# Four stored gates multiplied right after the conformer, and a fifth in its own projection

## The chip, the cores and the metric

The program runs on one core of one Trainium2 chip. The metric is the device time of one execution in microseconds, lower is better; it is given as the median of repeated runs. Matrix products run on TensorE (PE, its weight loads PEld), elementwise work on VectorE (DVE), ScalarE (ACT) and GpSimd (POOL), and nearly all transfers are issued by SyncE (SP), in one queue that is worked through in order. An engine executes its own instructions in order as well.

## What is computed

The reference is a trunk of two layers over 1024 latent tokens and 256 context tokens, 1024 channels wide. The change concerns the merge in layer 0, the even mixer:

```python
z, xbc, dt, glu, gate = split(h @ w_in, EVEN_SIZES)      # for the latents and for the context
ya = ssd_branch(z, xbc, dt, ...)                         # bidirectional Mamba-2
...
yb = conformer_conv(glu, cv_w, cv_b, cv_ln_g, cv_ln_b) * jax.nn.silu(gate)
return jnp.concatenate([ya, yb], axis=-1) @ w_out
```

`conformer_conv` is a gated depthwise convolution over time, a layer norm over the channels and a Silu. So `yb` is a product of two 1024-channel arrays over 1280 tokens: the conformer's result and the Silu of the gate's projection.

## The kernel before

All arrays of this stage stand channel-major: a tile of 128 channels by 1280 tokens (256 of the context, 1024 latents), eight tiles for 1024 channels. `SLICES` cuts the tokens into pieces of 512, 512 and 256. Matrix products are made in three passes of a high and a low part each (`zh`, `zl`, `hhi`, `hlo` and the like), so each weight is loaded raw, rounded on ACT into the high part (L158) and subtracted on DVE into the low part (L159).

`inproj0` does the in-projection of layer 0 and all that can be done beside it. A scheduler then sets the order of the instructions on each engine, and that order is fixed in the program. The parts that matter here, as the code has them:

- **The early gates.** The string `seq` interleaves the projections of the conformer's input (`glu`, whose convolutions run on POOL and DVE) with those of the SSD input and with five gates, channel tiles 4, 5, 6, 7 and 2 (`early`, L1270). Four stand in `seq`. `gate_early` (L1273 to L1280) projects a gate, takes its Silu on ACT (L1277) and stores it to DRAM, `gs_d` (L1278), because the conformer's result it belongs to does not exist yet.
- **The conformer** (L900 to L937) normalises the eight convolved tiles `cv` in place, slice after slice: mean, squares (POOL adds half of them, L922), the reciprocal root on POOL (`rstd_of`, L1544 and L1545), a product on DVE (L936) and the final Silu on ACT (L937). The eight tiles are done with the last of its slices. Its channel sum `csum` (L1321) lies in the one buffer of the pool `aq`, tag "accq", which the POOL convolutions used before.
- **The z blocks.** `zblocks((0, 1))` makes the first two column blocks of z beside the conformer; then comes the fifth early gate, `gate_early(2)`; then `ecf.close()` gives the memory of `aq` and of the conformer's pool back.
- **dt and the backward state.** `dt_prep` turns the dt columns into decays and stores two tables of rows, `rA_d` and `rB_d` (L1494). `ssd_back` walks ten chunks backwards: load the token-major chunk (`xtok`, 640 KB, L1508), weigh it on DVE (L1512), two matmuls (`bst`, L1532), the state `Hb` on POOL and DVE (L1528, L1536), and a store of each state (L1523).
- **The third z block**, `zblocks((2,))`: four weight quarters through two raw buffers (`wr`, L1150), split into a new pool `zp`, then ten token tiles of 24 matmuls (L171) each.
- **The last gates** (L1400). `gate(i)` runs for 3, 0, 1 and then for 4, 5, 6, 7, 2. The first three are projected: 72 matmuls, then per slice Silu (L1392), product (L1393), store to `yb_d` (L1394). For the five stored ones each slice is loaded from `gs_d` (L1385), multiplied on POOL (L1386) and stored to `yb_d` (L1387), through the four buffers of the tag "th". Between gates the raw weights `wb` of the out-projection are loaded (L1404).
- **The out-projection of layer 0.** It first reads the context's part of `yb_d` (`yl0`, L1407), splits eight weight tiles (`woh` on ACT, `wol` on DVE, `split_wo`), and multiplies (L1001) in step with the SSD chunks, whose row table `rB_d` is read into `rst` and copied on ACT (L1584).

The kernel's functions with the profile's line numbers:

Of the kernel before, what the change touches and what calls it, by code (L numbers as in the profile page):

```python
# [7 lines left out]
F32 = mybir.dt.float32  # L8
FR = mybir.dt.float32r
AF = mybir.ActivationFunctionType  # L10
ALU = mybir.AluOpType
# [3 lines left out]
P = 128  # L15
# [4 lines left out]
T = L + C  # L20
NT = T // P
SLICES = ((256, 768), (768, 1280), (0, 256))
# [88 lines left out]
class Kern:  # L111
# [1072 lines left out]
    def inproj0(self, hhi, hlo, cv, xbc_d, zs_d, gs_d, dtr, vwh, yb_d, xt_d, hb_d, s0, first):  # L1184
        tc, nc, A = self.tc, self.nc, self.A
        W = A["wch0"]
        e, wp, tq = self.e_in, self.wp, self.tq
        first, banks, emb = first
        ecf = ExitStack()
        aq = ecf.enter_context(self.pool(name="aq", bufs=1))  # L1190
# [19 lines left out]
        th = [[] for _ in range(8)]  # L1210
# [56 lines left out]

        order = [0, 1, 2, 3, 4, 5, 6, 7]
        seq = "gggggggxsxsxsxsxxxxxxxxg"
        early = (4, 5, 6, 7, 2)  # L1270
        g = x = ge = 0

        def gate_early(i):  # L1273

            def ev(ps, a, b):
                t = tq.tile([P, 512], F32, name="th", tag="th")
                nc.scalar.activation(t[:, :b - a], ps, AF.Silu)  # L1277
                nc.sync.dma_start(gs_d[i, :, a:b], t[:, :b - a])  # L1278

            self.proj_ch(wp, W[28 + i], hhi, hlo, ev)  # L1280
# [13 lines left out]
        em = ExitStack()  # L1294
# [29 lines left out]
            nc.gpsimd.tensor_tensor(csum[:, :T], csum[:, :T], cv[i][:, :T], op=ALU.add)  # L1324
        self.conformer(cv, csum, ecf)

        def token_major(xq, c, h):

            xc = xq.tile([P, 5, P], F32, name="xcT")
            nc.sync.dma_start(xc, xbc_d[5 * h:5 * h + 5, :, c * P:(c + 1) * P].rearrange("k p t -> p k t"))  # L1330
            xt = xq.tile([P, 5 * P], F32, name="xtok")
            for a, n in ((0, 3), (3, 2)):
                ps = self.bank("ms")
                for k in range(n):
                    nc.tensor.transpose(out=ps[:, k * P:(k + 1) * P], in_=xc[:, a + k], identity=self.ident)
                nc.scalar.copy(xt[:, a * P:(a + n) * P], ps[:, :n * P])
            nc.sync.dma_start(xt_d[c][:, 640 * h:640 * h + 640], xt)
# [31 lines left out]
                            nc.sync.dma_start(zs_d[t, :, 352 * j - 32:352 * j + 320], zs[:, :352])  # L1369
                assert not xq or not todo  # L1370

        zblocks((0, 1))
        gate_early(2)
        ecf.close()
        self.s0 = s0.__enter__()
        self.dt_prep(dtr)
        self.ssd_back(xt_d, hb_d)
        zblocks((2,))
        em.close()

        def gate(i):
            if i in early:
                for a, b in SLICES:
                    gt = tq.tile([P, 512], F32, name="gs", tag="th")
                    nc.sync.dma_start(gt[:, :b - a], gs_d[i, :, a:b])  # L1385
                    nc.gpsimd.tensor_tensor(gt[:, :b - a], cv[i][:, a:b], gt[:, :b - a], op=ALU.mult)  # L1386
                    nc.sync.dma_start(yb_d[a][i], gt[:, :b - a])  # L1387
                return

            def ev(ps, a, b):  # L1390
                gt = tq.tile([P, 512], F32, name="gs", tag="th")
                nc.scalar.activation(gt[:, :b - a], ps, AF.Silu)  # L1392
                nc.gpsimd.tensor_tensor(gt[:, :b - a], cv[i][:, a:b], gt[:, :b - a], op=ALU.mult)  # L1393
                nc.sync.dma_start(yb_d[a][i], gt[:, :b - a])  # L1394

            self.proj_ch(wp, W[28 + i], hhi, hlo, ev)

        ewl = self.ewl = ExitStack()
        wl = ewl.enter_context(self.pool(name="wl", bufs=1, side="right"))
        wb = [(k, wl.tile([P, D], F32, name=f"wb{k}", tag=f"wb{k}"), (wl, f"wb{k}")) for k in range(1, 8)]  # L1400
        for n, i in enumerate((3, 0, 1, 4, 5, 6, 7, 2)):
            gate(i)
            if n:
                nc.sync.dma_start(wb[n - 1][1], A["wout0"][8 + n])  # L1404
        we = ewl.enter_context(self.pool(name="we", bufs=1, side="right"))
        y = wl.tile([P, 8, P], F32, name="yl0", tag="wb0")
        nc.sync.dma_start(y, yb_d[256][:, :, :P].rearrange("k p t -> p k t"))  # L1407
# [271 lines left out]
```

## Time and profile before

| | us |
|---|---|
| three runs | 2196.39, 2198.22, 2204.89 |
| median | 2198.22 |
| the profiled execution | 2200.34 |
| its span | 2198.6 |
| PE busy | 2054.9 (93%) |
| PEld busy | 1630.2 (74%) |
| DVE busy | 1348.8 (61%) |
| ACT busy | 991.9 (45%) |
| POOL busy | 979.8 (45%) |

The profiled execution lies 2.1 us above the median of the runs, and 1.7 us of it lie outside its span. All times in the views count from the span's start. The shares are means over the whole span, in which stages with quite different limits follow each other; the stage around the change, from 540 to 1088 us, is read from the windows and timelines below. "Before <- X" in a row names what ended the engine's idle time ahead of the instruction.

### The profile page before, as it was taken

To read this page: it belongs to the slowest core of one execution; us is meant where nothing else is said; L and a number is where in the kernel's file an instruction comes from. 1 tells how busy PE (TensorE), PEld (TensorE's weight loads), DVE (VectorE), ACT (ScalarE), POOL (GpSimd) and SP (SyncE) were. 2 spreads that over 40 slices of the span, in tenths; PEclk is the share of its full clock that TensorE was granted. 3 is DMA by queue.
4 is the path that set the end of the run, shared out by engine and by line. 5 is a ranking of instruction groups with operands and counts; after the bars stand their busy time and mean duration, and the time that the engine had idled before them with its cause. 6 is when DMAs were issued, how large, how long until landed. Compare 5 with 4: busy or idle time off the path is not lost.

```text
span 2198.6 us, 28297 instructions
## 1 busy us (share of the span) xinstructions
PE 2054.9 (93%) x10636; PEld 1630.2 (74%) x10636; DVE 1348.8 (61%) x1889; ACT 991.9 (45%) x1549; POOL 979.8 (45%) x654
## 2 busy tenths in 40 slices
PE   7999999999979929999899999999999999899997
PEld 6888888889767716665488788888777676676675
DVE  6788896758445036667776321422566767676677
ACT  6455677533352122224234323233656767655510
POOL 0198999700112254546431113822445555434453
PEclk9999999999989969999899999999999999899998
DMA  8011122236637464464243422522311212534463
GB/s 306 30 39 39 51 79 85 96 129 213 218 106 250 169 221 149 146 214 157 98 159 125 134 70 82 179 99 80 99 49 51 59 52 57 159 92 126 122 182 130
DMA packets 158994, 269.33 MB, mean 123 GB/s; under 512 B 18901, under 2 KB 98385, under 8 KB 158601
## 3 DMA queue, kind: packets, MB, share of 16 engines
q1 hardware_dynamic: 157432, 264.01, 36.8%
q0 software_dynamic: 1280, 3.26, 0.5%
q8 instruction: 83, 1.36, 0.3%
q14 instruction: 55, 0.44, 0.1%
q10 hardware_dynamic: 144, 0.26, 0.0%
HBM read 189.82 MB, written 77.59 MB: 122 GB/s over the span
## 4 chain that ended last, share of the span: by engine, by line
PE 64%; POOL 13%; DVE 9%; ACT 6%; DMA 5%; issue 4%; SPq 0%; POOLq 0%; DVEq 0%; ACTq 0%
PE m L171 31%; PE m L1001 12%; POOL accq L1234 11%; PE po L738 3%; PE mz L1306 2%; PE po L1621 1%; PE m L832 1%; PE st L721 1%; PE st L720 1%; PE ms L208 1%; PE sg L1632 1%; ACT mv L664 1%; PE yd L1642 1%; ACT rb L425 1%; DVE wol L159 1%
## 5 line engine op out<-in xcount | busy, mean ns | idle before, releaser
L1234 POOL TENSOR_TENSOR accq<-accq,prod 128x1295 f32<-128x1295 f32 x90 | 287.7, 3197 | 33.9 <-ACT prod L1233 17.2
L171 PE MATMUL m<-hhi,wh 128*128 128x512 f32 (+1 forms) x792 | 280.9, 355 | 1.8 <-ACT th L1277 0.9
L171 PE MATMUL m<-hlo,wh 128*128 128x512 f32 (+1 forms) x792 | 280.6, 354 | 0.0
L171 PE MATMUL m<-hhi,wl 128*128 128x512 f32 (+1 forms) x792 | 280.2, 354 | 0.0
L1242 DVE SCALAR_TENSOR_TENSOR acc<-u,vwh,acc 128x1295 f32<-128x1295 f32 x150 | 235.2, 1568 | 12.9 <-ACT acc L1239 9.7
L731 POOL TENSOR_TENSOR pl<-pt,ph 128x512 fp32r<-128x512 f32 x96 | 130.1, 1356 | 198.9 <-ACT ph L730 195.9
L171 PE MATMUL m<-h1hi,wh 128*128 128x512 f32 (+1 forms) x544 | 213.3, 392 | 1.6 <-ACT rb L425 1.4
L171 PE MATMUL m<-h1lo,wh 128*128 128x512 f32 (+1 forms) x544 | 213.4, 392 | 0.0
L171 PE MATMUL m<-h1hi,wl 128*128 128x512 f32 (+1 forms) x544 | 212.3, 391 | 0.0
L1001 PE MATMUL m<-wol,yh 128*128 128x512 f32 x448 | 183.4, 409 | 4.6 <-DVE wol L954 2.5
L1001 PE MATMUL m<-woh,yh 128*128 128x512 f32 x448 | 185.9, 418 | 1.6 <-DVE t L1624 0.8
L1001 PE MATMUL m<-woh,ylo 128*128 128x512 f32 x448 | 181.6, 405 | 0.6 <-DVE ylo L159 0.6
L1233 ACT ACTIVATE prod<-u,vwh 128x1295 f32<-128x1295 f32 x90 | 124.1, 1382 | 97.9 <-POOL accq L1234 95.5
L171 PEld LDWEIGHTS m<-hhi,wh 128*128 128x128 f32 x792 | 149.7, 189 | 24.2 <-ACT th L1277 1.6
L171 PEld LDWEIGHTS m<-hhi,wl 128*128 128x128 f32 x792 | 149.7, 189 | 20.9
L171 PEld LDWEIGHTS m<-hlo,wh 128*128 128x128 f32 x792 | 149.8, 189 | 20.5
L730 ACT CAST ph<-pt 128x512 fp32r<-128x512 f32 x152 | 92.9, 619 | 97.6 <-PE po L738 86.2
L159 POOL TENSOR_TENSOR wl<-wr,wh 128x1024 fp32r<-128x1024 f32 x33 | 81.7, 2477 | 118.6 <-ACT wh L158 95.9
L738 PE MATMUL po<-ph,vs 128*66 128x512 f32 x304 | 121.6, 400 | 1.2 <-ACT ph L730 1.2
L171 PEld LDWEIGHTS m<-h1hi,wh 128*128 128x128 f32 x544 | 102.8, 189 | 22.6 <-ACT rb L425 2.0
L171 PEld LDWEIGHTS m<-h1hi,wl 128*128 128x128 f32 x544 | 102.9, 189 | 21.2
L171 PEld LDWEIGHTS m<-h1lo,wh 128*128 128x128 f32 x544 | 102.9, 189 | 19.9
(371 smaller groups left out, 4771.9 us busy)
## 6 DMA issues: line engine op xcount, KB each, us to landing
wr<-in_wch_dram SPq DMA_DIRECT2D x69, 512.0 KB
mw<-in_modw_dram SPq DMA_DIRECT2D x24, 512.0 KB
mr<-in_modw_dram SPq DMA_DIRECT2D x16, 512.0 KB
wor<-in_wout_dram SPq DMA_DIRECT2D x16, 512.0 KB
xbc_d<-acc SPq DMA_DIRECT2D x12, 640.0 KB
xcT<-xbc_d SPq DMA_DIRECT2D x20, 320.0 KB
xt_d<-xtok SPq DMA_DIRECT2D x20, 320.0 KB
xtok<-xt_d SPq DMA_DIRECT2D x10, 640.0 KB
```

Source lines behind the costliest of these rows:

```text
L159: (nc.gpsimd if pool_lo else nc.vector).tensor_tensor(lo, src, hi.bitcast(F32), op=ALU.subtract)
L171: nc.tensor.matmul(out, x(k), y(k), start=(c == 0), stop=(c == tot - 1))
L208: nc.tensor.matmul(ps[:4, :P], self.scond[:, n * h + k], w[j][:, k], start=(h + j + k == 0), stop=(h + j + k == halves + n - 1))
L425: nc.scalar.copy(tb[d, :n], ps[s])
L730: nc.scalar.copy(ph, p)
L731: (nc.gpsimd if x in (0, 1, 3) else nc.vector).tensor_tensor(pl, p, ph.bitcast(F32), op=ALU.subtract)
L738: nc.tensor.matmul(po[:66], vs[:, kb, v], p[y], start=first and i == 0, stop=last and i == 2)
L1001: nc.tensor.matmul(ps[f], y[u][:, k], w[k][v][:, 512 * f:512 * f + 512], start=i + j == 0, stop=i + j == 9)
L1233: nc.scalar.activation(pr, u[:, k:k + N], AF.Copy, scale=vwh[:, i, k:k + 1])
L1234: nc.gpsimd.tensor_tensor(acc, acc, pr, op=ALU.add)
L1242: nc.vector.scalar_tensor_tensor(acc[:, :N], u[:, k:k + N], vwh[:, i, k:k + 1], acc[:, :N], op0=ALU.mult, op1=ALU.add)
L1306: nc.tensor.matmul(mz[0][32 * g:32 * g + 2, P * c:P * c + P], self.scond32[:, 2 * k:2 * k + 2], w[:, k], start=k == 0, stop=k == 7)
```

## The change

Four stored gates (4, 5, 6, 7) are multiplied directly after the conformer, a whole channel tile at a time, in a tile `gse` that lies in the buffer of the tag "accq": one load of 640 KB, one POOL product over 1280 columns, three stores. Gate 2, still projected between the z blocks, is multiplied as gates 3, 0 and 1 are, and its Silu no longer goes through `gs_d`. The loop of the last gates keeps only 3, 0 and 1, and issues the `wb` loads behind them in groups.

```diff
-        early = (4, 5, 6, 7, 2)
+        early = (4, 5, 6, 7)
...
         self.conformer(cv, csum, ecf)
+
+        for i in early:
+            gt = aq.tile([P, 1295], F32, name="gse", tag="accq")
+            nc.sync.dma_start(gt[:, :T], gs_d[i])
+            nc.gpsimd.tensor_tensor(gt[:, :T], cv[i][:, :T], gt[:, :T], op=ALU.mult)
+            for a, b in SLICES:
+                nc.sync.dma_start(yb_d[a][i], gt[:, a:b])
...
+        def gate(i):
+            def ev(ps, a, b):
+                gt = tq.tile([P, 512], F32, name="gs", tag="th")
+                nc.scalar.activation(gt[:, :b - a], ps, AF.Silu)
+                nc.gpsimd.tensor_tensor(gt[:, :b - a], cv[i][:, a:b], gt[:, :b - a], op=ALU.mult)
+                nc.sync.dma_start(yb_d[a][i], gt[:, :b - a])
+
+            self.proj_ch(wp, W[28 + i], hhi, hlo, ev)
+
         zblocks((0, 1))
-        gate_early(2)
+        gate(2)
         ecf.close()
...
-        def gate(i):
-            if i in early:
-                for a, b in SLICES:
-                    gt = tq.tile([P, 512], F32, name="gs", tag="th")
-                    nc.sync.dma_start(gt[:, :b - a], gs_d[i, :, a:b])
-                    nc.gpsimd.tensor_tensor(gt[:, :b - a], cv[i][:, a:b], gt[:, :b - a], op=ALU.mult)
-                    nc.sync.dma_start(yb_d[a][i], gt[:, :b - a])
-                return
...
-        for n, i in enumerate((3, 0, 1, 4, 5, 6, 7, 2)):
+        k = 0
+        for i, m in ((3, 3), (0, 5), (1, 7)):
             gate(i)
-            if n:
-                nc.sync.dma_start(wb[n - 1][1], A["wout0"][8 + n])
+            for k in range(k, m):
+                nc.sync.dma_start(wb[k][1], A["wout0"][9 + k])
+            k = m
```

Behind the insertions the changed kernel's line numbers are higher: the load of `gse` is L1329, its product L1330, its stores L1332, gate's Silu, product and store are L1382 to L1384, and lines of the later functions are one higher than before. The scheduler's order changes in these places.

On SP's queue, between the row tables of `dt_prep` and the weight quarters of the third z block, before:

```order
L1494 DMA rA_d<-rt 96x10x128
L1494 DMA rB_d<-rt 96x10x128
L1508 DMA xtok<-xt_d 128x1280 x2
L1150 DMA wr<-in_wzdt_dram 128x704 x2
```

and now:

```order
L1495 DMA rA_d<-rt 96x10x128
L1329 DMA gse<-gs_d 128x1280
L1495 DMA rB_d<-rt 96x10x128
L1332 DMA yb_d<-gse 128x512 x2
L1332 DMA yb_d<-gse 128x256
L1509 DMA xtok<-xt_d 128x1280 x2
L1329 DMA gse<-gs_d 128x1280
L1509 DMA xtok<-xt_d 128x1280
L1524 DMA hb_d<-Hb 128x1024
L1332 DMA yb_d<-gse 128x512 x2
L1332 DMA yb_d<-gse 128x256
```

The third and fourth loads of `gse` and the stores of those two stand among the row tables and chunk loads; the first two loads stand earlier, and the last two weight quarters now follow all of these rows.

On POOL, from the conformer's last slice (`cacc`, `rs`, `crs`) to the backward states, before:

```order
L1544 TENSOR_SCALAR rs<-cvar 128x4
L1545 TENSOR_TENSOR crs<-rs,mhalf 128x4
L1528 TENSOR_TENSOR Hb<-Hb,expS 128x1024
L1311 MEMSET mrow 98x512
L1528 TENSOR_TENSOR Hb<-Hb,expS 128x1024 x7
```

and now (`u_782` is tile 2, `u_784` to `u_787` are tiles 4 to 7 of the conformer's result):

```order
L1383 TENSOR_TENSOR gs<-u_782,gs 128x512 x2
L1545 TENSOR_SCALAR rs<-cvar 128x4
L1546 TENSOR_TENSOR crs<-rs,mhalf 128x4
L1383 TENSOR_TENSOR gs<-u_782,gs 128x256
L1330 TENSOR_TENSOR gse<-u_784,gse 128x1280
L1330 TENSOR_TENSOR gse<-u_785,gse 128x1280
L1330 TENSOR_TENSOR gse<-u_786,gse 128x1280
L1330 TENSOR_TENSOR gse<-u_787,gse 128x1280
L1529 TENSOR_TENSOR Hb<-Hb,expS 128x1024 x4
```

Two products of gate 2 now stand ahead of the conformer's last reciprocal root, and the four whole-tile products ahead of the first backward state.

On ACT, the weights of the third z block with the semaphores that each waits for, before:

```order
L1493 COPY rt<-ms 96x256 [waits PE_49]
L158 CAST zh<-wr 128x704
L158 CAST zh<-wr 128x704 [waits DMAHW3_49]
L158 CAST zh<-wr 128x704 [waits DMAHW0_49]
L158 CAST zh<-wr 128x704 [waits DMAHW1_49]
```

and now:

```order
L1494 COPY rt<-ms 96x256 [waits PE_49]
L158 CAST zh<-wr 128x704 [waits DMAHW3_49,DMAHW5_49,DMAHW2_49,DMAHW6_49,DMAHW1_49,DMAHW7_49,DMAHW0_49,Pool_49]
L158 CAST zh<-wr 128x704
L158 CAST zh<-wr 128x704 [waits DMAHW5_49]
L158 CAST zh<-wr 128x704 [waits DMAHW7_49]
```

The pool `zp` of these weights lies in the memory that `ecf.close()` gives back, the buffer of `gse` among it, so the first cast now waits for POOL's last product on `gse` and for the stores that read it.

## Rows read from the trace of the kernel before

**Rows 1.** Busy time by windows: start:end, length, engines (xinstructions), clock, DMA share, GB/s

```profile
core 0: us, PE busy (x) PEld busy (x) DVE busy (x) ACT busy (x) POOL busy (x), PEclk, DMA share, GB/s
...
637.00:664.00 27.00, 13.42 (x80) 10.00 (x78) 13.06 (x31) 15.19 (x27) 0.00 (x0) 0.68 0.24 70
664.00:681.00 17.00, 16.22 (x85) 13.12 (x83) 7.57 (x9) 4.41 (x5) 2.37 (x2) 1.00 0.79 257
...
764.00:807.00 43.00, 2.05 (x16) 1.86 (x16) 1.65 (x1) 11.73 (x15) 19.88 (x19) 0.56 0.83 269
807.00:840.00 33.00, 29.32 (x116) 17.47 (x118) 30.04 (x31) 6.05 (x8) 19.11 (x8) 0.90 0.41 131
840.00:1018.00 178.00, 178.00 (x994) 115.24 (x990) 115.23 (x170) 52.91 (x75) 94.45 (x61) 1.00 0.51 169
1018.00:1088.00 70.00, 57.67 (x362) 31.35 (x362) 56.78 (x79) 19.75 (x32) 39.09 (x27) 0.88 0.37 123
```

**Rows 2.** Chain of waits that ended last, 755 to 832 us: start, us, what

```profile
765.47 4.68 DMA gs<-gs_d
...
771.26 4.25 DMA yb_d<-gs
...
784.28 2.91 DMA gs<-gs_d
...
788.64 2.36 DMA yb_d<-gs
```

**Rows 3.** Instructions of the tile gs: ns min/median/max, first and last start

```profile
L1386 POOL TENSOR_TENSOR gs<-u,gs x15: 724/1262/1263, 768.1 to 796.0; 128x512 f32<-128x512 f32 x10, 128x256 f32<-128x256 f32 x5
```

**Rows 4.** Timeline of ACT, 720 to 832 us: start, us, instruction [idle before]

```profile
722.30 0.47 ACT L1368 ACTIVATE zs<-m 128x352 f32<-128x352 f32 x1 [5.12 <-PE m L171]
...
763.65 0.38 ACT L1392 ACTIVATE gs<-m 128x256 f32<-128x256 f32 x1 [2.27 <-PE m L171]
...
796.71 6.72 ACT L158 CAST woh<-wb 128x1024 fp32r<-128x1024 f32 x7 [29.47 <-POOL gs L1386]
...
812.35 1.27 ACT L1584 CAST rows<-rst 111x1280 fp32r<-111x1280 f32 x1 [6.08 <-DMA rst<-rB_d]
```

**Rows 5.** Timeline of PE, 790 to 840 us, first out-projection matmuls

```profile
809.81 1.25 PE L1001 MATMUL m<-woh,yh 128*128 128x512 f32 x2
```

**Rows 6.** Timeline of ACT, 596 to 700 us

```profile
638.59 4.04 ACT L937 ACTIVATE u<-u,vecs 128x256 f32<-128x256 f32 x8 [3.13 <-DVE u L936]
...
661.63 1.46 ACT L158 CAST zh<-wr 128x704 fp32r<-128x704 f32 x2
671.42 1.63 ACT L158 CAST zh<-wr 128x704 fp32r<-128x704 f32 x2 [8.33 <-DMA wr<-in_wzdt_dram]
```

**Rows 7.** Timeline of POOL, 590 to 700 us

```profile
635.26 0.20 POOL L1544 TENSOR_SCALAR rs<-cvar 128x4 f32<-128x4 f32 x1 [13.33 <-ACT cvar L928]
...
696.67 1.90 POOL L1528 TENSOR_TENSOR Hb<-Hb,expS 128x1024 f32<-128x1024 f32 x1 [4.44 <-DVE Hb L1536]
```

**Rows 8.** Instructions of line 1234, the conformer's POOL convolutions

```profile
L1234 POOL TENSOR_TENSOR accq<-accq,prod x90: 2973/3003/4055, 101.3 to 403.1; 128x1295 f32<-128x1295 f32 x90
```

**Rows 9.** Timeline of all engines, 700 to 712 us: one chunk load and its use

```profile
704.54 0.32 SPq L1508 DMA_DIRECT2D xtok<-xt_d  x1
...
708.58 1.36 DVE L1512 TENSOR_TENSOR xtok<-xtok,wst 128x1024 f32<-128x1024 f32 x1 [1.76 <-DMA xtok<-xt_d]
```

**Rows 10.** Chain of waits that ended last, 630 to 690 us

```profile
665.16 7.09 DMA wr<-in_wzdt_dram
```

**Rows 11.** Timeline of PE, 612 to 723 us: the third z block

```profile
664.22 0.73 PE L171 MATMUL m<-zh,hhi 128*128 128x352 f32 x3
...
682.06 0.43 PE L171 MATMUL m<-zh,hhi 128*128 128x352 f32 x1 [1.60 <-ACT zs L1368]
...
701.83 1.02 PE L1532 MATMUL bst<-xtok 128*128 128x512 f32 x2
```

**Rows 12.** Timeline of DVE, 690 to 712 us

```profile
696.80 2.85 DVE L1512 TENSOR_TENSOR xtok<-xtok,wst 128x1024 f32<-128x1024 f32 x1 [0.26 <-DMA xtok<-xt_d]
```

More of the change, by code (lines that the diff above doesn't have):

```diff
@@ L1379, in inproj0 @@
         em.close()
-        def gate(i):
-            if i in early:
-                for a, b in SLICES:
-                    gt = tq.tile([P, 512], F32, name="gs", tag="th")
-                    nc.sync.dma_start(gt[:, :b - a], gs_d[i, :, a:b])
-                    nc.gpsimd.tensor_tensor(gt[:, :b - a], cv[i][:, a:b], gt[:, :b - a], op=ALU.mult)
-                    nc.sync.dma_start(yb_d[a][i], gt[:, :b - a])
-                return
[L1390 to L1396, printed above, removed]
         ewl = self.ewl = ExitStack()
```

## The prediction, made before the changed kernel was run

> **What bounds the kernel now.** PE is busy for 93% of the span, so I read first where it is not. The busy time by windows shows, around the change, four such stretches: 637 to 664 us (13.42 of 27 us busy), 764 to 807 (2.05 of 43), 807 to 840 (29.32 of 33, clock 0.90) and 1018 to 1088 (57.67 of 70); from 840 to 1018 PE works all 178.00 us [rows 1]. The change touches the first two.
>
> Then the chain of waits says what fills 764 to 807: a load of `gs`, a POOL product, a store to `yb_d` that frees a buffer, the next load [rows 2]. Fifteen products of 0.72 to 1.26 us run from 768.1 to 796.0 [rows 3]; POOL is busy for only 19.88 of the 43 us, the DMA share is 0.83 [rows 1]. It is a stage of transfers with the matrix engine standing by. On ACT its edges show: the last projected gate is read at 763.65, and the next work that matters, the `woh` casts, begins at 796.71 after 29.47 us of waiting for POOL's products [rows 4]. The first out-projection matmul is at 809.81 [rows 5]: 46.2 us after the last gate.
>
> By the order on PE, the changed kernel issues the same matmuls in the same order outside the stretch from the z blocks to the end of the SSD stage. So I work out by how much PE's idle time there moves, against the profiled execution of 2200.34 us.
>
> **What is removed.** Fifteen loads, products and stores at the end of the gates go. Of the 46.2 us there remains what the new order still needs between the last gate and the out-projection: the last product (0.72 us [rows 3]) with its store (2.36 to 4.25 us [rows 2]), the load of `yl0` (taken like a small load, 2.91 [rows 2]) and a cast (6.72/7 = 0.96 us [rows 4]). Much of that lies beside the casts of `woh`, whose first needs only weights loaded long before: 4.5 us remain of a possible 1 to 9. **Gain: 46.2 - 4.5 = about 41 us**, bounds 37 to 45. The out-projection's beginning also loses (33 - 29.32) = 3.7 us of idle time and 33 x (1 - 0.90) = 3.3 us to the low clock left by the idle stretch, in which the granted clock was 0.56 [rows 1]. The weights' DVE half stays, DVE being busy for 30.04 of the 33 us, so I take **3 us** of these 7, bounds 0 and 7.
>
> **What is added ahead of the conformer's end.** Two products of gate 2, 1.26 us each [rows 3], now stand on POOL before the reciprocal root `rs`, which started at 635.26 after 13.33 us of idle time [rows 7]. The first fits in that idle time; the second is made from a Silu finished just then, so `rs` is late by 0 to 1.3 us. I take **0.6**. Gate 2's transfers stay three stores, to `yb_d` in place of `gs_d`: nothing.
>
> **The four whole-tile products.** They share one buffer, so they go in rounds: product, three stores, landing, next load, landing, next product. The first needs channel tile 4 of the last slice: the eight Silus on ACT take 4.04 us from 638.59 [rows 6], the fifth is done at 638.59 + 5 x 0.505 = 641.1, with the 0.6 at 641.7. A product over 1280 columns took no row here; the POOL sum over 1295 columns took 2.97 to 4.06, median 3.00 [rows 8]: 3.0. It ends at 644.7. A round then costs: three issues of 0.32 us and the gaps, 1.05 [rows 9]; a store's landing of 2.36 to 4.25, taken 3.2 [rows 2]; the load of 640 KB; the product, 3.0. The load has its like in the chunk loads of the same size, issued at 704.54 and used at 708.58: 4.0, with 0.3 for waiting to issue, 4.3 [rows 9]. Sum 1.05 + 3.2 + 4.3 + 3.0 = **11.6 us**. Bounds: below 9.3, with 2.36, 2.91 and 2.97; above, a weight quarter of 352 KB took 7.09 us where loads crowd [rows 10], so 640 KB would take about 13, and a round about 22. I stay near the value in the middle, since the chunk load has the same size and shape, but add 3 us for the third round, which meets two chunk loads on SP's queue.
>
> Three rounds and 3 us end at 644.7 + 34.8 + 3 = 682.5, the last stores at 682.5 + 1.05 + 3.2 = 686.7.
>
> **What waits for that.** POOL's first `Hb` product and, on SP, the row tables and chunk loads stand behind these steps, but the one that ends on PE is ACT's cast of the third z block's weights: its memory is the buffer of `gse`, so it waits for the last store. Before, it ran at 661.63 [rows 6], and z began at 664.22 [rows 11]. Now the cast is at about 687 and **z begins at 688** (678 to 697).
>
> It does not all count, because the backward states do not wait for z and three of their steps move ahead of it. The two later weight quarters are loaded only once the first two are split; taking 7 us for load and split and 1.6 for the casts (7.09 [rows 10], 1.63 [rows 6]), the first three token tiles, which must wait for them in their second half (36 matmuls of 0.16 us, 5.8 us), end at 688 + 7 + 1.6 + 5.8 = 702.4. Before, the other seven tiles ran from 682.06 to the last read at 722.30 [rows 11, 4], 40.2 us: 168 matmuls of 0.16 us and seven state steps of twice 0.95 us (1.02 for the two overlapping matmuls of a half [rows 11]), 26.9 + 13.3. Now four such steps remain: 26.9 + 7.6 = 34.5. z ends at 737, **15 us later**. The three projected gates took 763.65 - 722.30 = 41.35 us [rows 4] and end at 778.4; the out-projection begins at about 783 instead of 809.8, 27 us earlier.
>
> **The sum:** -27 - 3 = -30 us, of which the 15 us of the z delay are the price, with the 0.6 inside them. 2200.34 - 30 = 2170; the profiled execution stands 2.1 us above the median of the runs, so I forecast **2168**.
>
> Where a rule bears on it: while POOL multiplied `Hb` at 696.67 for 1.90 us [rows 7], DVE's product of two arrays in SBUF, begun at 696.80, took 2.85 us [rows 12] against 1.36 elsewhere [rows 9]. So the whole-tile products, 3 us each, can hold up `dt_prep`'s DVE work by up to 12 us in all. I cost that at nothing, since z waits until 687 for the last store in any case and the row tables' last copies stood ahead of the cast at 661.63 [rows 6]; with quick rounds this cover shrinks, and some 5 us of it would show. The Trainium skill, "SBUF — State Buffer", section "Who interferes with whom", says that a DVE instruction with two SBUF inputs and a GpSimd one that reads SBUF take turns at a shared port, each for its whole length. That row agrees; by the rule alone four products would cost DVE four full lengths, and the sum would be -30 + 12 = -18 if nothing covered them.
>
> **Rivals.**
> - *Quick rounds.* If the DMA queues are as free as in the window 637 to 664 (share 0.24 [rows 1]), a round costs its lower bound of 9.3 us and the third meets nothing: z at about 677, 11 us earlier, 2157. Against it: 664 to 681 has a share of 0.79 [rows 1], and chunk loads now fall between the rounds. Chance 0.12. The Trainium skill, "DMA: Bandwidth & Descriptors", section "Anatomy of one DMA — SWDGE (gpsimd) path", fits a transfer as 2.0 us and its bytes at 436 GB/s; by my estimate from it, 3.5 us for 640 KB and 2.6 for a store of 256 KB make a round of 10.1, near this rival. The rows are slower than that: 2.91 to 4.68 for a load of 256 KB or less [rows 2].
> - *The SSD chain sets the end.* The chunks' row table was copied at 812.35 [rows 4], 15.6 us after POOL came free of the products at 796.7. Without them POOL is free at about 779 and the copy comes at about 796, 16 us earlier, not 30. If this chain, not PE, paces the stage up to 1088 us, where PE shows idle time [rows 1], the gain is 16 us: 2182. Against it: 178 us of full PE work lie between [rows 1]. Chance 0.14.
> - *Slow rounds: no gain, or slower.* One mechanism turns the sign: the stores and loads of `gse` crowd with the chunk loads, so that a round takes 22 us as by the weight quarter's row [rows 10]. z would then begin at 644.7 + 3 x 22 + 5 = 716 and the gates would end 43 us late; that eats the 44 us. The point at which it turns slower is a round of about 22 us, and at 26 it is slower by 11 us: 2210. For it: the share of 0.83 and landings of over 4 us under `gs` traffic [rows 1, 2]. Against it: at most one `gse` transfer in flight and its size twin's 4.0 us [rows 9]. Chances 0.08 for no change, 0.04 for slower.
>
> **How the numbers follow.** My own case has 0.62. A difference under 0.5%, 11 us, can hardly be told from none with this kernel. My case (2160 to 2177 by the bounds of z's start and of the casts), quick rounds (2157) and the SSD chain (2182) are faster by more: 0.88. Within 0.5%: 0.08. Slower: 0.04. The range goes from 2155, quick rounds with 2 us more of the clock's share, to 2186, the SSD chain with a slightly slow round; it leaves out about 0.15.
>
> **What the profile after would show.** Right: no products between the last gate and `woh`, an idle stretch of PE of under 10 us there, PE idle from about 662 to 688 but for three state steps, the `zh` cast waiting for a `yb_d` store, four POOL products about 12 us apart, and 840 to 1018 unchanged but earlier. Wrong would be: a new wait of the out-projection for `yl0` or `wb`; the SSD chain's idle time growing by what the gates saved; rounds of 9 or of 20 us; or the conformer's end more than 2 us late.

## The result, and the profile after

| | before | after |
|---|---|---|
| median of the runs, us | 2198.22 | 2168.45 (2166.31 to 2172.58) |
| ratio to before, 95% interval | | 0.9862 [0.9846, 0.9878] |
| span of the profiled execution, us | 2198.6 | 2166.3 |
| PE busy, us | 2054.9 (93%) | 2054.0 (95%) |
| last projected gate read | 763.65 [rows 4] | 787.82 |
| first out-projection matmul (L1001) | 809.81 [rows 5] | 790.54 |
| first matmul of the next stage (L1050) | 1105.3 | 1076.3 |

The total was forecast within a microsecond. Two terms of the sum were not: they were off by 8 and 7 us in opposite directions, so the total is right by luck. PE's busy time is 0.9 us shorter, its span 32.3: nearly the whole gain is idle time.

On ACT (timeline, 630 to 800 us; start, length, instruction, idle before) the gates now run straight into the out-projection:

```profile
640.20 4.04 ACT L937 ACTIVATE u<-u,vecs 128x256 f32<-128x256 f32 x8 [4.02 <-DVE u L936]
...
689.80 1.46 ACT L158 CAST zh<-wr 128x704 fp32r<-128x704 f32 x2 [22.35 <-DMA yb_d<-gse]
...
710.40 1.18 ACT L1375 ACTIVATE zs<-m 128x352 f32<-128x352 f32 x3
...
745.59 0.47 ACT L1375 ACTIVATE zs<-m 128x352 f32<-128x352 f32 x1 [3.38 <-PE m L171]
...
786.87 1.04 ACT L158 CAST yh<-yl 128x1024 fp32r<-128x1024 f32 x1 [2.23 <-DMA yl<-yb_d]
787.82 0.38 ACT L1382 ACTIVATE gs<-m 128x256 f32<-128x256 f32 x1
...
789.04 6.75 ACT L158 CAST woh<-wb 128x1024 fp32r<-128x1024 f32 x7
```

The 29.47 us of waiting ahead of the `woh` casts [rows 4] are gone. In their place stand 22.35 us ahead of `zh`, until the last store of `gse`. Another change: `yl0` (cast at 786.87) is there before the last gate's last slice is read. It reads the first of the three slices of every gate (`yb_d[256]`, latent tokens, and not the context's part, as the section on the kernel before has it). The last gate's first slice is now stored before its other two; before, the gate that was last was a stored one, at the end of the products. From the last gate to L1001 remain 2.7 us of 46.2.

The four products on POOL (timeline) and SP's queue between them:

```profile
635.91 1.27 POOL L1383 TENSOR_TENSOR gs<-u,gs 128x512 f32<-128x512 f32 x1 [4.52 <-ACT cvar L928]
637.26 0.32 POOL L1545 TENSOR_SCALAR rs<-cvar 128x4 f32<-128x4 f32 x1
...
642.84 2.89 POOL L1330 TENSOR_TENSOR gse<-u,gse 128x1280 f32<-128x1280 f32 x1 [0.25 <-ACT u L937]
652.82 2.88 POOL L1330 TENSOR_TENSOR gse<-u,gse 128x1280 f32<-128x1280 f32 x1 [7.09 <-DMA gse<-gs_d]
668.43 2.88 POOL L1330 TENSOR_TENSOR gse<-u,gse 128x1280 f32<-128x1280 f32 x1 [12.72 <-DMA gse<-gs_d]
680.37 2.92 POOL L1330 TENSOR_TENSOR gse<-u,gse 128x1280 f32<-128x1280 f32 x1 [9.07 <-DMA gse<-gs_d]
```

```profile
655.73 1.28 SPq L1332 DMA_DIRECT2D yb_d<-gse  x3
661.65 0.33 SPq L1495 DMA_DIRECT2D rA_d<-rt  x1
662.10 0.49 SPq L1329 DMA_DIRECT2D gse<-gs_d  x1
667.48 0.32 SPq L1495 DMA_DIRECT2D rB_d<-rt  x1
```

The rounds take 10.0, 15.6 and 11.9 us. In the first and third rounds the next load was issued 1.9 and 2.1 us after the last store had been (648.91, 674.69). In the second the stores were issued by 657.0, but the third load stands on SP behind `rA_d`, which waits for ACT until 661.65: it was issued after 5.1 us, 3 us later than in the other rounds, and then took 6.17 us itself. The chain of waits (start, us, what) has the rest, and the two DVE instructions that met a product on POOL:

```profile
642.97 3.11 DVE pp__5616 L1436
...
653.36 2.70 DVE wst L1472
...
662.10 6.17 DMA gse<-gs_d
...
684.91 4.74 DMA yb_d<-gse
```

PE (timeline) does three state steps of four matmuls each, with waits, and only then z, whose run holds the other six steps:

```profile
678.01 6.03 PE L1533 MATMUL bst<-xtok 128*128 128x512 f32 x8 [7.88 <-DVE xtok L1513]
688.74 3.78 PE L1533 MATMUL bst<-xtok 128*128 128x512 f32 x4 [4.70 <-DVE Hb L1537]
691.53 1.73 PE L171 MATMUL m<-zh,hhi 128*128 128x352 f32 x3
...
698.39 1.88 PE L1533 MATMUL bst<-xtok 128*128 128x512 f32 x4
...
703.00 1.02 PE L1533 MATMUL bst<-xtok 128*128 128x512 f32 x2
```

From L1001 to L1050 took 295.5 us before and takes 285.8 now. In the windows that follow (start:end, length, then busy time of PE, PEld, DVE, ACT, POOL, clock, DMA share, GB/s), first before, then after:

```profile
809.81:839.81 30.00, 26.33 (x108) 16.05 (x108) 27.26 (x30) 6.05 (x8) 16.30 (x8) 0.94 0.45 142
839.81:1069.81 230.00, 220.74 (x1244) 138.65 (x1242) 159.37 (x226) 68.27 (x99) 124.97 (x80) 0.98 0.48 162
1069.81:1105.30 35.49, 32.43 (x199) 22.20 (x200) 25.65 (x40) 9.85 (x15) 12.46 (x13) 0.91 0.30 106
```

```profile
790.54:820.54 30.00, 28.73 (x114) 19.80 (x112) 22.11 (x28) 12.58 (x15) 13.56 (x8) 1.00 0.72 234
820.54:1050.54 230.00, 223.97 (x1297) 139.91 (x1298) 165.00 (x241) 71.89 (x107) 131.92 (x87) 0.97 0.50 168
1050.54:1076.30 25.76, 22.56 (x139) 17.15 (x138) 19.07 (x26) 6.88 (x10) 7.94 (x9) 0.98 0.34 123
```

PE's idle time there falls from 295.49 - 279.50 = 16.0 us to 285.76 - 275.26 = 10.5, and its busy time by 4.2 (the granted clock at the beginning 1.00 for 0.94, at the end 0.98 for 0.91; these are means of its two levels, 1.00 at 2.4 GHz and 0.50 at 1.2).

### The profile page after: what moved, and what is told of

It reads as the page before. It is cut to its first block, busy times and chain, and to the rows that moved or that the text cites. A ratio compares the mean times of both kernels' runs of the same rounds, so it can differ in the third digit from the quotient of the medians.

```text
span 2166.3 us, 28270 instructions
## 1 busy us (share of the span) xinstructions
PE 2054.0 (95%) x10636; PEld 1632.4 (75%) x10636; DVE 1343.5 (62%) x1889; ACT 990.8 (46%) x1549; POOL 976.7 (45%) x646
## 3 DMA queue, kind: packets, MB, share of 16 engines
q0 software_dynamic: 1280, 3.26, 0.5%
## 4 chain that ended last, share of the span: by engine, by line
PE 62%; POOL 14%; DVE 8%; DMA 6%; ACT 6%; issue 4%; SPq 1%; POOLq 0%; DVEq 0%; ACTq 0%
PE m L171 29%; PE m L1001 12%; POOL accq L1234 11%; PE po L738 4%; PE mz L1306 2%; PE po L1622 1%; PE m L832 1%; PE st L721 1%; PE st L720 1%; PE sg L1633 1%; ACT mv L664 1%; PE ms L208 1%; PE yd L1643 1%; ACT rb L425 1%; PE m L1109 1%
## 5 line engine op out<-in xcount | busy, mean ns | idle before, releaser
L1001 PE MATMUL m<-wol,yh 128*128 128x512 f32 x448 | 182.4, 407 | 1.3 <-DVE wol L954 1.1
L1001 PE MATMUL m<-woh,ylo 128*128 128x512 f32 x448 | 182.7, 408 | 0.5 <-DVE ylo L159 0.5
L1001 PE MATMUL m<-woh,yh 128*128 128x512 f32 x448 | 181.8, 409 | 1.1 <-DVE t L1625 0.8
```

Of the source, the lines that this page charges most:

```text
L1001: nc.tensor.matmul(ps[f], y[u][:, k], w[k][v][:, 512 * f:512 * f + 512], start=i + j == 0, stop=i + j == 9)
```

## The experiments

All are read against the kernel before, measured beside them (2199.1 to 2200.1 us). "First z" is the first matmul of the third z block, "stretch" the time from the first L1001 to the first L1050, in the one profiled execution of each kernel. The next two columns are PE's idle time and its mean granted clock in the stretch. "Ahead" counts, in the trace, the out-projection matmuls (L1001) that stand in PE's order ahead of the first SSD matmul (`ms<-tmp,xt`). For comparison, before: 295.5 us, 16.0 idle, clock 0.96, 0 ahead; changed: 285.8, 10.5, 0.98, 44 ahead. The diffs are against the changed kernel, for e11 against the kernel before.

| run | median us | ratio, 95% | first z | last gate | first L1001 | stretch | PE idle in it | clock | ahead |
|---|---|---|---|---|---|---|---|---|---|
| e1_gate2 | 2192.97 | 0.9969 [0.9954, 0.9983] | 666.9 | 766.8 | 806.6 | 295.8 | 12.2 | 0.94 | 0 |
| e2_four | 2202.01 | 1.0010 [0.9995, 1.0025] | 689.4 | 784.8 | 801.9 | 307.0 | 20.1 | 0.94 | 2 |
| e4a_one_buf | 2167.36 | 0.9848 [0.9826, 0.9871] | 690.7 | 784.0 | 786.8 | 285.9 | 12.5 | 0.99 | 44 |
| e4d_four_buf | 2177.51 | 0.9898 [0.9872, 0.9924] | 691.0 | 791.3 | 794.0 | 291.2 | 8.5 | 0.94 | 44 |
| e5_inplace | 2156.37 | 0.9818 [0.9796, 0.9841] | 672.0 | 774.6 | 777.3 | 286.3 | 9.0 | 0.97 | 44 |
| e5_inplace_dve | 2157.50 | 0.9813 [0.9791, 0.9834] | 670.7 | 775.0 | 777.7 | 291.3 | 8.2 | 0.94 | 44 |
| e8a_first | 2167.42 | 0.9862 [0.9846, 0.9879] | 664.9 | 783.0 | 785.7 | 289.6 | 10.9 | 0.96 | 44 |
| e9_late_y0 | 2199.54 | 1.0001 [0.9992, 1.0011] | 690.9 | 786.7 | 807.4 | 296.3 | 15.6 | 0.95 | 0 |
| e10_first_inplace | 2161.76 | 0.9822 [0.9808, 0.9837] | 664.8 | 778.3 | 781.0 | 286.7 | 10.8 | 0.97 | 44 |
| e11_slice_major | 2195.00 | 0.9974 [0.9961, 0.9988] | 664.7 | 764.8 | 802.6 | 304.2 | 16.2 | 0.94 | 26 |

### The two parts alone

**e1_gate2**: gate 2 is multiplied at once; the other four are loaded and multiplied at the end, as before.

```diff
-        for i in early:
-            gt = aq.tile([P, 1295], F32, name="gse", tag="accq")
...
+        for n, i in enumerate((3, 0, 1, 4, 5, 6, 7, 2)):
+            if i != 2:
+                gate(i)
```

> Gate 2 alone is multiplied at once between the z blocks; the four stored gates stay at the end of the gates. My theory: the 33 us between the last gate and the woh casts are worked through in proportion to their fifteen slices, so twelve slices take 26 us, and the kernel gains 6.6 us less the 1.6 us by which the conformer's end came later in the changed kernel: about 2193 us, last POOL product at about 790 us. Rival: other transfers (out-projection weights, inputs of the next stage) fill that stage anyway; then the last product stays within 2 us of 796 and the time within 2 us of 2198. The third z block should begin at 664 to 667 us.

**e2_four**: the four tiles follow the conformer; gate 2 is stored and multiplied at the end.

```diff
-        early = (4, 5, 6, 7)
+        early = (4, 5, 6, 7, 2)
...
-        gate(2)
+        gate_early(2)
...
+            if i not in (4, 5, 6, 7):
+                gate(i)
```

> The four whole-tile products follow the conformer, but gate 2 is stored and multiplied after the last projected gate as before. My theory: the parts add up, so this one gains the changed kernel's 29.8 us less the 5 us of gate 2: about 2174 us, with some 8 us from the last projected gate's Silu to the first woh cast. Rival: one gate costs nearly as much at the end as a whole chain of load, product and store, 10 us and more: 2178 us or above. If instead the three slices are hidden, 2168 us.

The first came out as expected: 7 us by the medians. In its trace the time from the last gate to the first `woh` cast (793.46) is 26.7 us for 33.1, where 26 was expected; as the gates end 3.1 us later, L1050 comes 2.9 us earlier. The second did not come out: 2174 us was expected, and the four early products alone gain nothing. The parts don't add up (7 us gained and nothing, against 30 together). In e2 ACT's and PE's timelines show part of the reason:

```profile
784.76 0.38 ACT L1399 ACTIVATE gs<-m 128x256 f32<-128x256 f32 x1 [2.27 <-PE m L171]
793.28 6.72 ACT L158 CAST woh<-wb 128x1024 fp32r<-128x1024 f32 x7 [4.93 <-POOL gs L1393]
...
800.85 1.99 ACT L158 CAST yh<-yl 128x1024 fp32r<-128x1024 f32 x2
```

```profile
801.94 1.22 PE L1001 MATMUL m<-woh,yh 128*128 128x512 f32 x2 [14.22 <-ACT yh L158]
```

Three slices of one stored gate still stand between the last gate and `woh`, and PE comes to L1001 17 us after the gates. That is 29 us less than before. But the last gate comes 21 us later (784.8 for 763.65), as in the changed kernel, and the stretch behind L1001 is 11 us longer, 307 us: L1050 comes 3.6 us later than before. So the gain does not go by the number of products. What makes the stretch so long is taken up below, and stays open.

### What holds the third z block

The prediction had z wait for `zh`, whose memory is the buffer of `gse`. **e4a_one_buf** gives `gse` a buffer of its own, in a pool opened behind gate 2, where the program now has the products too, so `zh` need not wait. **e4d_four_buf** is the same with `bufs=4`, so there are no rounds.

```diff
+        gp = ecf.enter_context(self.pool(name="gp", bufs=1))
+        for i in early:
+            gt = gp.tile([P, 1280], F32, name="gse")
```

> One buffer of its own for the whole-tile products, in memory that the third z block's weights do not take, so that their first cast does not wait for the last store. The rounds stay, and PE's order still has three backward-state steps ahead of z. Theory A (as predicted): the wait for the memory is what holds z; without it the first cast comes at about 668 us and z at about 672, the gates end 15 us or more earlier: 2153 us. Theory B: with that wait gone z is held at nearly the same time by the state steps ahead of it on PE, whose second and third need Hb from POOL behind the fourth product and chunks from SP behind the stores: z within 4 us of 691, time within 4 us of 2168.

> Four buffers of their own: the four loads go out together and there are no rounds; z stands ahead of the state steps on PE again and its weights wait for none of it. My theory: the rounds and what hangs on them cost the changed kernel about 20 us in z; without them the products are done by 665 us, z begins at 666 to 672 us and the out-projection at about 774 instead of 790.5: 2152 us. Rival, the shared port: four products back to back on POOL stop DVE's work on dt for up to 12 us, the row tables come at 672 us or later, z as late: 2158 to 2162 us. Rival, order: the gain is under 5 us because the state chain, not z, sets the time: 2164 us or more.

In e4a the cast came 24 us earlier (ACT), and z hardly (PE):

```profile
666.17 1.46 ACT L158 CAST zh<-wr 128x704 fp32r<-128x704 f32 x2
697.29 0.78 ACT L158 CAST zh<-wr 128x704 fp32r<-128x704 f32 x1 [29.66 <-DMA wr<-in_wzdt_dram]
```

```profile
687.91 3.78 PE L1533 MATMUL bst<-xtok 128*128 128x512 f32 x4 [4.52 <-DVE Hb L1537]
690.71 1.87 PE L171 MATMUL m<-zh,hhi 128*128 128x352 f32 x3
```

So the memory of `gse` is not the only thing that holds z. PE's order has three state steps ahead of it, the second and third need `Hb` from POOL, and POOL's first `Hb` stands behind the fourth product; the chunk loads and the third weight quarter stand on SP behind the stores of `gse`. All of it waits for the rounds, by more than one way. This is the expectation's theory B, in z and in the time.

In e4d, for which 2152 us was expected, the products were through by 653.5, and z was hardly earlier either; the kernel was 9 us slower than the changed one. The chain of waits names what came in:

```profile
656.61 0.04 POOLq L1421
656.65 0.59 issue
657.24 3.52 DMA rows<-in_rows_dram
...
663.10 2.16 DVE z L1431
```

The small vectors of `dt_prep` (`rows`, L1421, issued by POOL at 620.63 in the changed kernel) now came only after the last product and the landing of a `yb_d` store. The four buffers had, by this wait, taken memory that `rows` needed, and the whole of `dt_prep` slid some 20 us: its last copies of the row tables are at 687.08 (666.56 in the changed kernel), the `zh` cast at 687.87. A wait on reused memory was replaced by another.

**e5_inplace** writes the product over the conformer's tile and stores from there, so that a `gse` buffer is free after its product, not after its stores. **e5_inplace_dve** also does the products on DVE, which ought to end the slowed instructions of `dt_prep`.

```diff
-            nc.gpsimd.tensor_tensor(gt[:, :T], cv[i][:, :T], gt[:, :T], op=ALU.mult)
+            nc.gpsimd.tensor_tensor(cv[i][:, :T], cv[i][:, :T], gt[:, :T], op=ALU.mult)
...
-                nc.sync.dma_start(yb_d[a][i], gt[:, a:b])
+                nc.sync.dma_start(yb_d[a][i], cv[i][:, a:b])
```

```diff
-            nc.gpsimd.tensor_tensor(cv[i][:, :T], cv[i][:, :T], gt[:, :T], op=ALU.mult)
+            nc.vector.tensor_tensor(cv[i][:, :T], cv[i][:, :T], gt[:, :T], op=ALU.mult)
```

> The changed kernel with its product written over the conformer's tile, so that the stores read that tile and the one gate buffer is free as soon as the product ends. A round is then load and product, 4.0 to 6.2 us and 2.9 us, in place of 10 to 15.6 us; and in the order on PE z stands ahead of the backward states again. Theory A (z's start sets the time by way of the rounds): the fourth product ends at 668 to 673 us, z begins at 670 to 676 instead of 691.5, the gates end 13 us or more earlier: 2152 to 2156 us. Theory B (another thing sets the time, the states or the dt chain): under 5 us gained, 2164 us or more. In between, 2157 to 2163, if the four products stop DVE's dt work for longer than the changed kernel's do.

> As the last, but with the four products on DVE. If DVE and POOL took turns at a shared port in the changed kernel (two DVE operations of 0.5 us took 3.11 and 2.69 us beside the whole-tile products), then with nothing on POOL no DVE operation of the dt work takes over 0.6 us, the row table rB_d is issued at 662 to 665 us instead of 667.5, and the four products take 1.5 us each. z at 666 to 671 us, 2146 to 2150 us. Rival: the long DVE times came from something else (the operands' memory, DMA traffic); then they stay with the products on DVE, and the time is that of the last kernel within 2 us.

e5_inplace did what was expected, with 2156.37 us a little over the upper end of theory A, and beats both kernels. Its products (instructions of the tile) and its cast (ACT):

```profile
L1330 POOL TENSOR_TENSOR u<-u,gse x4: 2877/2885/2889, 642.5 to 668.3; 128x1280 f32<-128x1280 f32 x4
```

```profile
671.21 1.47 ACT L158 CAST zh<-wr 128x704 fp32r<-128x704 f32 x2 [3.52 <-POOL u L1330]
```

Three rounds now take 25.8 us for 37.5, the cast waits for the last product and for no store, and z stands ahead of the state steps in PE's order again. z begins 19.5 us earlier and the out-projection 13.2. On DVE the products take 1.48 to 1.49 us, and the instructions of L1436 and L1472 that took 3.11 and 2.69 us take about 0.5 again. So POOL and DVE did hold each other up. Yet z began only 1.4 us earlier, and the time is the same, not the 2146 to 2150 us expected: the second copies of the row tables then waited 5.29 us for the store of `rA_d`. One wait was taken away and another came in its place; what the holding up costs by itself is not shown.

### What the out-projection gained

Its stretch is 9.7 us shorter, where 3 were forecast. The kernel before reads `yl0` late. DVE then makes its low half `ylo` late as well, and the low halves of the eight weight tiles (`wol`) follow it. In the kernel before, the first and the last of these instructions were, on DVE (timeline):

```profile
805.35 2.69 DVE L159 TENSOR_TENSOR ylo<-yl,yh 128x1024 fp32r<-128x1024 f32 x1 [41.64 <-ACT yh L158]
...
827.72 1.21 DVE L159 TENSOR_TENSOR wol<-xl,woh 128x1024 fp32r<-128x1024 f32 x1
```

**e9_late_y0** is the changed kernel with one more load into `yl0`, from the last slice, ahead of the real one, so that `yl0` waits for the last gate's last store and for that load.

```diff
         y = wl.tile([P, 8, P], F32, name="yl0", tag="wb0")
+        nc.sync.dma_start(y, yb_d[0][:, :, :P].rearrange("k p t -> p k t"))
```

> The changed kernel, but the out-projection's first load (yl0) waits for the last slice of the last gate, as it did in the kernel before; it reads another slice first, whose result is not used. The first out-projection matmul comes at about 803 us instead of 790.5. Theory A (the out-projection's start loses time wherever the weights' split and the first SSD chunk fall together, 296 to 307 us from its first matmul to the next stage in the kernels with a late start, 286 in the changed one): that stretch grows by 8 us or more and the time is 2186 us or above. Theory B (it is only shifted, or the wait is hidden): the stretch stays within 3 us of 286 or shrinks, and the time is 2181 us or below.

It gives back the whole gain of the change, as theory A had it. z and the gates are where they were, L1001 is 16.8 us later, and the stretch is 296.3 us. Not all of the delay is the wait for the slice: on SP the added load is issued at 793.73 and the real one at 802.25, so 8.5 us of it are the added load itself. The run shows what it costs when `yl0` comes late, not how late the order of before made it. DVE (timeline) shows how the second part may come about; below it the first 30 us of the stretch:

```profile
807.35 1.23 DVE L159 TENSOR_TENSOR ylo<-yl,yh 128x1024 fp32r<-128x1024 f32 x1 [20.63 <-ACT yh L158]
808.49 0.68 DVE L1578 COPY Hf<-ms 128x512 f32<-128x512 f32 x1
809.09 1.22 DVE L159 TENSOR_TENSOR wol<-wb,woh 128x1024 fp32r<-128x1024 f32 x1
```

```profile
807.37:837.37 30.00, 26.36 (x110) 17.05 (x111) 29.18 (x32) 6.13 (x8) 14.01 (x7) 0.83 0.45 140
```

DVE's `ylo` stands ahead of the eight `wol` in its order, so a late `yl0` holds the weights' low halves too, though `woh` is long cast. They then fall among the SSD's work: DVE is busy for 29.18 of the 30 us, in the changed kernel for 22.11, where `wol` runs from 790.14, most of it while POOL waits. That row has a mean granted clock of 0.83, so in part at the level of 1.2 GHz, after some 20 us with little work on PE. And the added load changed more than `yl0`: in PE's order the first SSD matmuls now stand ahead of the out-projection, while in the changed kernel 44 of its matmuls come first (PE, changed kernel, then e9):

```profile
801.30 1.98 PE L1575 MATMUL ms<-tmp,xt 128*128 128x512 f32 x4
```

```profile
802.39 3.47 PE L1576 MATMUL ms<-tmp,xt 128*128 128x512 f32 x4 [12.78 <-POOL tmp L1569]
```

**e11_slice_major** is the kernel before, with the stored gates multiplied slice by slice over the five gates, so that `yl0`'s slice is complete early.

```diff
+        for sl in SLICES:
+            for i in early:
+                gate(i, (sl,))
```

> The kernel before, with the stored gates' fifteen slices at the end taken slice by slice over the five gates: the slices that the out-projection's first load reads are stored after five products, not after thirteen, and the weights' casts still wait for the last product. Theory A (that first load, by way of the cast behind it and of the weights' low parts on DVE, is what costs at the out-projection's start): the load has landed before the last product, the first out-projection matmul comes 2 to 4 us after the first woh cast instead of 13, and the stretch from it to the next stage is 286 to 291 us instead of 295.5: 2182 to 2188 us. Theory B (the casts' wait for the last product is what counts): within 4 us of 2198.

L1001 followed `woh` by 1.1 us, as the theory of the late `yl0` had it. But the products themselves end at 801.4, the stretch is 304 us where that theory had 286 to 291, and the kernel gained 5 us only, which lies in the range of theory B. PE waits for the products, and the stretch then begins at a low clock:

```profile
764.00:790.00 26.00, 2.75 (x22) 2.36 (x21) 0.00 (x0) 2.52 (x5) 11.91 (x10) 0.63 0.84 270
790.00:840.00 50.00, 35.78 (x134) 23.66 (x134) 30.98 (x33) 15.36 (x18) 23.74 (x15) 0.78 0.60 190
```

An early `yl0` is thus not enough. Over all the runs, the kernels whose PE comes straight from the gates have a stretch of 286 to 291 us, those with a stall ahead of L1001 one of 295 to 307. But the same line parts them by PE's order: in the traces the changed kernel and the six with 286 to 291 us have one order in the stretch, as far as their records go, with 44 out-projection matmuls ahead of the SSD; each of the others has another order, no two the same (the last column counts how each begins). The scheduler made these orders, and no run holds the order fixed while it moves `yl0` or the stall. So three things go together in every run, the late split on DVE, the low clock after a stall and the order on PE, and what each has of the 9.7 us is not shown.

Among the kernels with one order, what parts 286 from 291 can be read from the table: PE's idle time is 8 to 13 us in all, but the granted clock is 0.97 to 0.99 at 286 us, 0.96 at 290 and 0.94 at 291. Most of the difference lies in the last 36 us, with a clock of 0.76 in e4d, 0.75 in e5_inplace_dve and 0.85 to 0.94 in the others. It moves between executions of one kernel too: those of e5_inplace_dve took 2150.21 us at a mean granted clock of 0.985 and 2160.83 at 0.976, and the latter is the one with the profile. Why it fell was not tried.

### Another place for the products

**e8a_first** does nothing after the conformer and puts the four stored gates first in the last loop, ahead of gates 3, 0 and 1, so that z is not delayed. **e10_first_inplace** is the same with the product in place.

```diff
+        for n, i in enumerate((4, 5, 6, 7, 3, 0, 1, 2)):
+            if i != 2:
+                gate(i)
```

> Nothing follows the conformer: gate 2 is multiplied at once, and the four stored gates stand ahead of the three projected ones in the last loop, in the four small buffers as before. Theory A: the stall is a matter of where the twelve slices stand; beside PE's 41 us of projected gates they cost only what the first projected gate's Silu waits for a buffer, 3 to 8 us, and z begins at 667 as in the kernel before: 2150 to 2156 us. Theory B: the projected gates wait for the buffers and for POOL's products in order, PE stands still for 15 us or more in the gates: 2163 us or more.

> The last but two's order (nothing after the conformer, gate 2 at once, the four stored gates ahead of the projected ones), with each stored slice's product written over the conformer's tile, so that its small buffer is free after the product and not after the store. Theory A: what held the first projected gate there was the buffers, each kept for a load, a product and a store's landing (PE lost 16 us between 723 and 764); without the landing the twelve slices are done by 745 us and PE loses under 5 us in the gates: the out-projection starts at 769 to 774 us, 2146 to 2152 us. Theory B: the loads are bounded by DMA traffic, not by the buffers; PE still loses 10 us or more there: 2158 us or above.

z begins at 665 in both, and the delay returns at the gates, as the theories B had it. In e8a (ACT; then windows) gate 3 finds its buffers taken:

```profile
751.93 0.60 ACT L1383 ACTIVATE gs<-m 128x512 f32<-128x512 f32 x1 [14.72 <-DMA yb_d<-gs]
```

```profile
723.00:764.00 41.00, 24.67 (x112) 20.60 (x111) 1.23 (x1) 3.23 (x6) 18.35 (x16) 0.79 0.74 253
```

PE loses 16.3 of these 41 us, in e10 9.6 (31.37 busy; theory B had 10 or more), where the chain shows `gs` loads of 8.53 and 4.71 us. e8a equals the changed kernel. e10 was expected at 2146 to 2152 us, below e5_inplace, and is not: its median is 5 us above, which the spread of both does not part from none (2159.53 to 2163.94 us, e5_inplace 2153.28 to 2165.0). The transfers of the stored gates cost PE time in this place too, and beside the conformer's tail much of it is idle anyway [rows 1].

## Why the prediction was right, and where it was not

- **The gap at the gates, 41 us.** Right: 46.2 - 2.7 = 43.5, within 37 to 45. The rest of 4.5 was too high because `yl0` no longer waits for the last slice; the prediction had its whole chain of product, store and load still to come.
- **z's delay, 15 us.** This step failed: 23.3 at z's last read, 24.2 at the last gate. Of the missing 9 us, 3.5 are the start of z (688 forecast, 691.53). The rounds were right in sum, 37.5 us for 37.8, though unlike in size: the second and not the third was long, 3 us by the place of a load on SP's queue and the rest by that load's own length. Over the forecast were the last stores, landing in 4.74 us where 3.2 were taken, after 1.6 us of issuing for 1.05, and the step that named ACT's cast as "the one that ends on PE": by e4a the state steps ahead of z end as late. Another 4.5 us are the run to the first three reads, 691.53 to 710.40, 18.9 us for 14.4. The working put no state step into it; two and a half of the remaining six lie there, at 1.9 us each, and at the end of it PE waits for ACT, whose first read stands behind a weight cast (708.05). It had subtracted three steps from the later seven, though two of those three had stood in the first stretch before. From 710.40 on it was nearly right: 35.2 us for 34.5, and the gates 42.2 for 41.35.
- **The out-projection's beginning, 3 us.** This step failed in the other direction: 9.7, outside its bounds of 0 to 7. The step read 30.04 busy us of DVE [rows 1] and kept them. They were no fixed work of that window: in the changed kernel DVE is busy for 22.11 of its first 30 us, since the `wol` lie ahead of the SSD's work there. And it expected the time from 840 to 1018 "unchanged but earlier", while PE's order in it changed. Of the 9.7 us, 5.5 are idle time of PE and 4.2 busy time, at a clock of 0.98 for 0.96. By e9 and e11 an early `yl0` goes with the gain but does not bring it alone; how much of it is the split, the clock or the order stays open.
- **The sum.** -19.3 (forecast -27) and -9.7 (forecast -3) make -29.0 at L1050, forecast -30. The total was right because a delay forecast 9 us too short and a gain forecast 7 us too small nearly cancel (the rest of the gates' gap, 2.7 for 4.5, does the remainder); that is luck, it was not right by its steps. The spans of the two profiled executions differ by 32.3 us; the other 3.3 lie behind L1050, where nothing was tried, and the execution before stood 2.1 us above its median.
- **The conformer, 0.6 us.** It is 1.6, over the bound of 1.3. `rs` is 2.0 us late: 1.3 by the product, as bounded, and the rest goes with ACT's timeline, where a Silu of gate 2 (635.24) now stands ahead of the variance copy (635.73) that `rs` reads.
- **The held-up DVE work at no cost.** e5_inplace_dve does not speak against it, but it takes the products off POOL in the in-place kernel and brings in another wait, so it does not show it either. The lengths are as the Trainium skill, "SBUF — State Buffer", section "Who interferes with whom", would have them: 3.11 and 2.69 us beside products of 2.9. The price by that rule alone, a sum of -18, did not show: L1050 came 29.0 us earlier.
- **The rivals.** Quick rounds: the first took 10.0 us, the others did not. The SSD chain as the bound: refuted, its row table was cast at 808.34, 4 us earlier than [rows 4], and L1050 came 29 us earlier (its sum was also off: 779 + 15.6 is 794.6, not 796). Slow rounds: none took over 15.6.

## What to carry to other kernels

Ask of a load which producer it really waits for, and what stands behind its first user on each in-order engine: here one slice of one gate held eight weight splits that did not need it. In e9 one late load gives back the gain of the whole change, by its wait and by all that the scheduler then ordered otherwise. So before two runs are read against each other in a stage, compare the order of their instructions in it. If a moved step uses one buffer in rounds, free it by its last reader on an engine, not by its stores: writing the product in place was worth another 10 to 12 us (by the ratios and by the medians). Before taking more memory instead, look at who gets that memory next.

## What the runs showed that was not expected

- A load of 640 KB took about 3.9 us from issue (648.91) to product when little else ran, and 6.17 at 662.10 under other transfers; with weight loads beside them, loads of 256 KB or less took 4.71 and 8.53 us (e10). The Trainium skill, "DMA: Bandwidth & Descriptors", section "Anatomy of one DMA — SWDGE (gpsimd) path", fits a transfer that GpSimd issues as 2.0 us and its bytes at 436 GB/s, by my estimate 3.5 us for 640 KB and 2.6 for 256. These were issued by SP; the first is near the fit, the others lie far above it.
- One load that waits in SP's queue behind a store not yet ready was issued about 3 us later than its like in the other rounds (5.1 us after the last store's issue, for 1.9 and 2.1), and nothing in the waiting engines' rows says so: POOL's row names the load, and only SP's timeline shows when it was issued.
- Four whole-tile products take 2.9 us each on POOL and 1.5 on DVE, for the same end of the kernel.
